# Output projection of a hybrid attention layer: gate folded into the weights, scale and shift in one VectorE instruction, three group-norm steps moved from GpSimd to VectorE

## The chip, the cores and the metric

The kernel runs on one core of one Trainium2 chip. The metric is the device time of one execution in microseconds (us); lower is better. Besides the time, one execution is recorded by the hardware profiler, and all rows below come from that record.

## The reference, cut to what matters

One layer: attention and retention heads are computed from a projected input, their outputs are concatenated and projected by `w_out`, the result is gated and added to the input, and the sum is normalised, modulated and sent to a mixture of experts.

```python
def _ret_output(o, gn_g, gn_b, gate, dtype):
    mu = jnp.mean(o, axis=-1, keepdims=True)
    var = jnp.mean(jnp.square(o - mu), axis=-1, keepdims=True)
    on = (o - mu) * lax.rsqrt(var + EPS)
    on = jnp.transpose(on, (0, 2, 1, 3)).reshape(B, L, H * dv).astype(dtype)
    return (on * gn_g + gn_b) * jax.nn.silu(gate)
...
    x_new = x + gt1 * (jnp.concatenate([attn_x, ret_x], axis=-1) @ w_out[l])
    h2 = _modulate(_rmsnorm(x_new, norm2_g[l]), sh2, sc2)
    y = _hier_moe(h2..., ...)
    x_new = x_new + gt2 * y
```

2048 tokens, width 1024, 4 retention heads of 128 values, 8 attention heads of 64, 32 experts in 4 groups of which each token takes two.

## The kernel before, in words

Everything is float32. Tokens lie on the 128 partitions, so there are 16 token tiles. Matrix products are made of three passes on rounded parts (high by high, high by low, low by high).

There are four stages. The first projects the input. The second (`phase2`, some 545 to 1268 us in the record) is attention: 288 steps, each with score products on TensorE, an exponential and a cast on ScalarE (ACT), a subtraction shared by VectorE (DVE) and GpSimd (POOL) (line 950), row maxima on DVE for units that come later (lines 900 and 905), and the products with the values. Its instruction order is written out by hand. Every third step it also takes one step of `fillers`, which prepares the third stage: it loads the modulation rows into `mod2` (gate, shift, scale; `mod2[:, 0]` is the gate gt1), loads `w_out` in 16 pieces of 128x512, splits each into a high and a low part (ACT line 1015, DVE line 1016), scans the retention states, loads constants, and runs the cross part of retention for token tile 0 (`cross_ahead`).

The third stage (`phase3`, 1268 to 1556 us) is the output projection with the second norm and the router. For each of the 16 tiles and each half of 512 columns, `wout` makes 24 matmuls into PSUM, multiplies the result by the gate (DVE line 1255, into a scratch tile `y3`) and adds it to `x` (DVE line 1256). `squares` takes the sum of squares on ACT (line 1277), `scaled` multiplies `x` by the norm's gain and modulation on DVE (line 1273, into `xa`). `norm2` computes the reciprocal root on small columns, multiplies `xa` by it on ACT (line 1283), adds the shift on POOL (line 1284) and stores `h2`. `h2_T` transposes `xa` on TensorE (line 1291) and copies it from PSUM on ACT (line 1292); `router` multiplies it by the router weights (line 1296); for every second tile `route` picks the experts of two tiles with some forty small DVE instructions (lines 1308 to 1373) and two on ACT (lines 1316 and 1349), then POOL scatters the choices into lists in memory (line 1376).

Beside that, two tiles ahead, `ret_cross` finishes the retention of a tile: a product on TensorE (line 1161), an addition and statistics on DVE, a normalisation by four ACT instructions (line 1176), and then three steps on POOL: times the gain (line 1180), plus the bias (line 1182), times the gate `gs` (line 1184). `mix_T` transposes the result for the projection of the next tile (line 1242).

Work of the third stage is put into slots (`self.at`, `self.flush`), and a scheduler orders the instructions of each engine when the program is built; on the chip each engine takes its own in that fixed order. PSUM tiles of the name `pr` share three buffers: the two transposes of `h2_T`, one of `mix_T` and the retention product follow each other through them. The SBUF tiles of the stage are reserved in a fixed order, `y3` third among them (two buffers of 2 KB per partition), on the space that the second stage leaves. SP issues nearly all loads and stores, in order.

The fourth stage computes the experts from 1589 us on. It starts from the lists and from `h2`.

Of the kernel before, what the change touches and what calls it, by code (L numbers as in the profile page):

```python
# [11 lines left out]
F32 = mybir.dt.float32  # L12
F32R = mybir.dt.float32r
F16 = mybir.dt.float16
I32 = mybir.dt.int32
AF = mybir.ActivationFunctionType
ALU = mybir.AluOpType
# [4 lines left out]
P = 128  # L22
D = 1024
KD = D // P
# [44 lines left out]
RING3 = {"qr": 3, "st": 3, "ro": 4, "gs3": 3, "bs": 1, "x3": 3}  # L69
# [63 lines left out]
class Build:  # L133
# [657 lines left out]
    def phase2(self):  # L791
# [10 lines left out]
        with tc.tile_pool(name="kv", bufs=1, reuse_waits="tile") as kv, tc.tile_pool(name="p2", bufs=2, reuse_waits="tile") as pool, \  # L802
# [186 lines left out]
            def fillers():  # L989

                g = self.mod2
                for j, dst in enumerate((g[:, 0, :], g[:, 1, :], g[:, 2, :], self.gt2)):
                    nc.sync.dma_start(dst, self.bcast(self.mod_d[:, j * D:(j + 1) * D], D))
                for j in range(2):
                    s_ = slice(j * 512, (j + 1) * 512)
                    n2 = p.tile([P, 512], F32, name="n2", tag="wa2", bufs=4)
                    nc.sync.dma_start(n2, self.bcast(a["norm2_g"][:, s_], 512))
                    yield
                    yield
                    nc.vector.scalar_tensor_tensor(g[:, 2, s_], g[:, 2, s_], 1.0, n2, op0=ALU.add, op1=ALU.mult)  # L1000
                pieces = [(k, n) for k in range(KD) for n in range(2)]
                raws = []
                for q in range(len(pieces) + 2):
                    if q < len(pieces):
                        k, n = pieces[q]
                        raw = p.tile([P, 512], F32, name="wor", tag="wa2", bufs=4)
                        nc.sync.dma_start(raw, a["w_out"][0, k * P:(k + 1) * P, n * 512:(n + 1) * 512])
                        raws.append(raw)
                    yield
                    if q < 2:  # L1010
                        continue
                    k, n = pieces[q - 2]
                    raw = raws[q - 2]
                    s_ = slice(n * 512, (n + 1) * 512)
                    nc.scalar.copy(self.wohi[:, k, s_], raw)
                    nc.vector.tensor_sub(self.wolo[:, k, s_], raw, self.wohi[:, k, s_])
                    yield

                gch = p.tile([P, RH], F32, name="gch", bufs=1)
                nc.scalar.activation(gch, self.gam[:, 8:12], AF.Exp, scale=float(P))  # L1020
                us = []
                for n in range(NT + 2):
                    if n < NT:
                        u = p.tile([P, RH, RV], F32, name="su", tag="wa2", bufs=4)
                        nc.sync.dma_start(u[0:64].rearrange("p h d -> p (h d)"), self.st_d[n, 0:64])
                        nc.sync.dma_start(u[64:128].rearrange("p h d -> p (h d)"), self.st_d[NT - 1 - n, 64:128])
                        us.append(u)
                    yield
                    if n < 3:
                        continue  # L1030
                    n -= 2
                    for h in range(RH):
                        nc.vector.scalar_tensor_tensor(us[n][:, h, :], us[n - 1][:, h, :], gch[:, h:h + 1], us[n][:, h, :], op0=ALU.mult, op1=ALU.add)
                    nc.sync.dma_start(self.st_d[n, 0:64], us[n][0:64].rearrange("p h d -> p (h d)"))
                    nc.sync.dma_start(self.st_d[NT - 1 - n, 64:128], us[n][64:128].rearrange("p h d -> p (h d)"))
                    yield

                for dst, src in ((self.list_d, a["slot_init"]), (self.acc_d[L:], a["zeros"]), (self.h2_d[L:], a["zeros"])):
                    nc.sync.dma_start(dst, src)
                    yield  # L1040
                for _ in self.constants3(p):
                    yield
                for t in range(AHEAD):
                    yield from self.cross_ahead(p, ps, t)
# [108 lines left out]
        nc.vector.tensor_mul(qx, pq, self.consts3[0])  # L1153
        return qx

    def ret_cross(self, alloc, psr, qx, st, o, gs):

        nc, gng = self.nc, self.consts3[1]
        pc = psr("pc3", [P, RH, RV])
        for h in range(RH):  # L1160
            nc.tensor.matmul(pc[:, h, :], qx[:, h, :], st[:, h, :], start=True, stop=True)
        nc.vector.tensor_add(o, pc, o)
        yield
        bs = alloc("bs", [P, RH, 6])
        mv = alloc("mv", [P, 5, RH, 2])
        for h in range(RH):
            nc.vector.bn_stats(bs[:, h, :], o[:, h, :])
        yield
        for h in range(RH):
            nc.vector.bn_aggr(mv[:, 0, h, :], bs[:, h, :])  # L1170
        rsqrt = self.rsqrt_steps(mv[:, 1, :, 0], mv[:, 0, :, 1], 1.0, (mv[:, 2, :, 0], mv[:, 3, :, 0]))
        yield from rsqrt
        nc.vector.scalar_tensor_tensor(mv[:, 4, :, 0], mv[:, 0, :, 0], -1.0, mv[:, 1, :, 0], op0=ALU.mult, op1=ALU.mult)
        yield
        for h in range(RH):
            nc.scalar.activation(o[:, h, :], o[:, h, :], AF.Identity, bias=mv[:, 4, h, 0:1], scale=mv[:, 1, h, 0:1])
            if h % 2:
                yield
        of = o.rearrange("p h d -> p (h d)")
        nc.gpsimd.tensor_mul(of, of, gng[:, 0, :])  # L1180
        yield
        nc.gpsimd.tensor_add(of, of, gng[:, 1, :])
        yield
        nc.gpsimd.tensor_mul(of, of, gs)

    def cross_ahead(self, p, ps, t):

        def alloc(name, shape, dt=F32):
            if name == "ro":
                return self.c3.tile(shape, dt, name=f"ro{t}")  # L1190
            if name in ("bs", "mv"):
                return p.tile(shape, dt, name=name, bufs=1)
            return p.tile(shape, dt, name=name, tag="wa2", bufs=4)

        def psr(name, shape, dt=F32):
            return ps.tile(shape, dt, name=name, tag="nm")

        qr, st, o, gs = self.ret_load(alloc, t)
        yield
        yield  # L1200
        qx = self.ret_T(alloc, psr, qr)
        yield
        yield from self.ret_cross(alloc, psr, qx, st, o, gs)
        self.crossed.append(o)
        yield

    def phase3(self):
        nc, tc, a = self.nc, self.tc, self.a
        with tc.tile_pool(name="p3", bufs=2, reuse_waits="tile") as pool, tc.tile_pool(name="ps3", bufs=2, space=PSUM, reuse_waits="tile") as ps:
            wr, br, ri, before, one16, run = self.consts3[2:]  # L1210

            p = Reserved(pool)
            for name, cols, dt in (("h2", D, F32), ("h2T", (KD, P), F32), ("y3", 512, F32), ("mThi", (KD, P), F32R), ("mTlo", (KD, P), F32R), ("xa", D, F32),
                                   ("x3", D, F32), ("qx", (RH, P), F32), ("mx3", H * HD, F32), ("qr", (RH, 2, HD), F32), ("st", (RH, RV), F32),
                                   ("ro", (RH, RV), F32), ("gs3", RH * RV, F32), ("en", (2, 2, 2), I32), ("ad", (2, 2), I32)):
                p.reserve(name, [P, *cols] if isinstance(cols, tuple) else [P, cols], dt, bufs=RING3.get(name, 2))
# [30 lines left out]
            def wout(hi, lo, n, x):  # L1247
                o = ps.tile([P, 512], F32, name="pw", tag="pw", bufs=3)
                for k in range(KD):
                    for i, (l, r) in enumerate(((hi, whi), (hi, wlo), (lo, whi))):  # L1250
                        ins = nc.tensor.matmul(o, l[:, k, :], r[:, k, n * 512:(n + 1) * 512], start=(k == 0 and i == 0), stop=(k == KD - 1 and i == 2))
                self.flush()
                s_ = slice(n * 512, (n + 1) * 512)
                y = p.tile([P, 512], F32, name="y3", bufs=RING3.get("y3", 2))
                nc.vector.tensor_mul(y, o, self.mod2[:, 0, s_])
                nc.vector.tensor_add(x[:, s_], y, x[:, s_])

            def shift_logits():

# [19 lines left out]
            def norm2(t, x, xa, h2, ss):  # L1279
                nc.sync.dma_start(self.acc_d[t * P:(t + 1) * P, :], x)  # L1280
                nc.vector.tensor_add(ss[:, 0:1], ss[:, 4:5], ss[:, 5:6])
                self.rsqrt(ss[:, 1:2], ss[:, 0:1], 1.0 / D, (ss[:, 2:3], ss[:, 3:4]))
                nc.scalar.activation(h2, xa, AF.Copy, scale=ss[:, 1:2])
                nc.gpsimd.tensor_add(h2, h2, self.mod2[:, 1, :])
                nc.sync.dma_start(self.h2_d[t * P:(t + 1) * P, :], h2)

            def h2_T(h2, h2T, half):
# [101 lines left out]

            def stage_cross(t):  # L1390
                if t < NT:
                    for _ in self.ret_cross(alloc, psr, R.pop((t, "qx")), *R[t][1:4]):
                        pass

            def stage_mix(t, half):
# [668 lines left out]
```

## Time and profile before

| what | us |
|---|---|
| median of 3 runs | 2432.54 |
| lowest and highest of them | 2430.21, 2434.29 |
| the profiled execution | 2424.75 |
| its span, first to last instruction | 2423.0 |
| third stage, of that span | 1268 to 1556 |
| from there to the first expert work on TensorE | 1556 to 1589 |

PE is TensorE's matmuls, PEld its weight loads, SPq the queue of SP. In a row of the timeline the first number is the start, the second the duration, both in us; what stands in brackets at its end is the idle time of that engine before it and what ended it. In a group of instructions the two numbers after the bar are the busy time in us and the mean duration in ns, those after the second bar the idle time before. L1284 is line 1284 of the kernel before.

### The profile page before, as it was taken

What the parts mean: (1) busy time and instruction counts of PE and PEld (TensorE: products, weight loads), DVE (VectorE), ACT (ScalarE), POOL (GpSimd) and SP (SyncE); (2) the same over time, 40 slices, a digit from 0 to 9 for tenths busy, and PEclk for the clock granted to TensorE, in tenths of its full rate; (3) what the DMA queues carried; (4) which work ended last, traced back from release to release, by engine and by line L of the source; (5) the groups of instructions that cost most, each with busy time, mean ns of one, the idle gap of its engine ahead of it and who ended that gap; (6) DMA issues with size and microseconds to landing.
All of it is one profiled execution on the core that took longest, in us unless ns stands there. A gap on an engine that the chain in (4) does not pass through costs nothing. (4 is left out here: it accounts for less than half of the span.)

```text
span 2423.0 us, 46706 instructions
## 1 busy us (share of the span) xinstructions
PE 2268.9 (94%) x16778; PEld 1835.5 (76%) x16778; DVE 1862.3 (77%) x3449; ACT 1510.5 (62%) x2179; POOL 951.3 (39%) x943
## 2 busy tenths in 40 slices
PE   7899999999999999999999998769999999999992
PEld 3788888886788877878877777557888787778872
DVE  6655555556888989998967888758878988887786
ACT  3533333333899999999984333345756766665663
POOL 2544444442455565556564445312232212121221
PEclk8999999998999999999999999889999999999996
DMA  7333444448011122223118544177887998897887
GB/s 273 104 111 113 116 118 118 118 134 221 24 41 41 45 54 58 63 60 99 31 64 268 156 150 136 73 227 253 296 299 260 361 332 302 316 358 236 281 296 294
DMA packets 221685, 417.88 MB, mean 172 GB/s; under 512 B 63931, under 2 KB 115427, under 8 KB 220211
## 3 DMA queue, kind: packets, MB, share of 16 engines
q1 hardware_dynamic: 186002, 363.00, 43.5%
q0 software_dynamic: 26672, 51.04, 9.0%
q8 instruction: 162, 2.65, 0.4%
q10 hardware_dynamic: 8736, 0.27, 0.2%
q14 instruction: 113, 0.92, 0.1%
HBM read 336.97 MB, written 86.23 MB: 175 GB/s over the span
## 5 line engine op out<-in xcount | busy, mean ns | idle before, releaser
L1536 DVE TENSOR_TENSOR wlo<-wraw,whi 128x1024 fp32r<-128x1024 f32 x384 | 460.0, 1246 | 28.4 <-ACT whi L1535 7.0
L950 POOL TENSOR_TENSOR pl<-p,ph 128x512 f16<-128x512 f32 x288 | 339.1, 1178 | 303.2 <-DVE pl L950 222.2
L1535 ACT CAST whi<-wraw 128x1024 fp32r<-128x1024 f32 x384 | 382.4, 1052 | 31.7 <-DMA wraw<-in_moe_w_gate 9.7
L905 DVE TENSOR_REDUCE mx<-sm 128x1 f32<-128x512 f32 x512 | 345.0, 685 | 62.9 <-PE sm L904 61.8
L1599 PE MATMUL gu<-whi,xT 128*128 128x512 f32 x1024 | 326.7, 395 | 5.9 <-DVE xT L1591 2.8
L938 ACT ACTIVATE p<-st,cexp 128x1024 f32<-128x1024 f32 x288 | 320.7, 1113 | 17.2 <-PE st L936 8.4
L942 ACT CAST ph<-p 128x1024 f16<-128x1024 f32 x288 | 301.6, 1047 | 7.5
L434 PE MATMUL pp<-whi,hT_hi 128*128 128x512 f32 (+1 forms) x688 | 263.1, 382 | 5.5 <-ACT v L625 3.3
L965 PEld LDWEIGHTS <-ph 128*128 128x128 f16 x4608 | 218.2, 97 | 65.7 <-issue 60.5
L434 PE MATMUL pp<-whi,hT_lo 128*128 128x512 f32 (+1 forms) x688 | 256.3, 373 | 2.7 <-POOL hT_lo L413 1.5
L434 PE MATMUL pp<-wlo,hT_hi 128*128 128x512 f32 (+1 forms) x688 | 255.1, 371 | 0.9 <-DVE wlo L388 0.9
L965 PE MATMUL o<-vx,ph 128*128 128x65 f16 (+1 forms) x4608 | 252.1, 194 | 1.3 <-ACT ob L971 1.2
L965 PE MATMUL o<-vx,pl 128*128 128x65 f16 x2304 | 239.8, 192 | 0.0
L904 PE MATMUL sm<-KHL,qhh 128*128 128x512 f32 x512 | 230.4, 455 | 5.6 <-DVE mx L905 2.8
L935 PE MATMUL st<-qhh,KHL 128*128 128x512 f32 x576 | 231.6, 402 | 1.0 <-ACT p L938 0.2
L1599 PEld LDWEIGHTS gu<-whi,xT 128*128 128x128 f32 x1024 | 193.9, 189 | 50.2 <-issue 6.1
L936 PE MATMUL st<-qlm,KO 65*128 65x512 f32 x576 | 231.8, 402 | 0.1
L1599 PE MATMUL Y<-whi,hT 128*128 128x512 f32 x624 | 216.8, 403 | 9.8 <-DVEq L1589 3.3
L950 DVE TENSOR_TENSOR pl<-p,ph 128x514 f16<-128x514 f32 x288 | 212.0, 736 | 15.9 <-ACT ph L942 11.2
L965 PEld LDWEIGHTS <-pl 128*128 128x128 f16 x2304 | 214.2, 99 | 0.0
L1599 PE MATMUL gu<-wlo,xT 128*128 128x512 f32 x512 | 200.7, 392 | 0.0
L1661 POOL DMA_INDIRECT acc_d<-y,slots x31 | 67.7, 2185 | 223.0 <-DVE y L1647 120.7
(354 smaller groups left out, 4610.0 us busy)
## 6 DMA issues: line engine op xcount, KB each, us to landing
wraw<-in_moe_w_gate SPq DMA_DIRECT2D x128, 512.0 KB
wraw<-in_moe_w_up SPq DMA_DIRECT2D x128, 512.0 KB
wraw<-in_moe_w_down SPq DMA_DIRECT2D x128, 512.0 KB
wa<-in_w_ada SPq DMA_DIRECT2D x64, 256.0 KB
wa<-in_w_ada SPq DMA_DIRECT2D x8, 1024.0 KB
wraw<-in_w_in SPq DMA_DIRECT2D x32, 256.0 KB
xt<-in_x SPq DMA_DIRECT2D x16, 512.0 KB
qh_d<-qt SPq DMA_DIRECT2D x64, 128.0 KB
```

The costliest lines, as they stand in the source:

```text
L434: ins = nc.tensor.matmul(out[:, :n], l[:, k, :], r[:, k, c0:c0 + n], start=(k == 0 and i == 0), stop=(k == KD - 1 and i == 2))
L904: nc.tensor.matmul(sm, qhh[:, h0 + h, j * P:(j + 1) * P], khl[g][:, n * 512:(n + 1) * 512], start=True, stop=True)
L905: nc.vector.reduce_max(mx[u][:, 2 * h + j, n:n + 1], sm, axis=AX.X)
L935: nc.tensor.matmul(st[:, n, :], khl[g][:, kt * P:(kt + 1) * P], qh, start=True, stop=False)
L936: nc.tensor.matmul(st[:, n, :], ko[g][:, kt * P:(kt + 1) * P], ql, start=False, stop=True)
L938: nc.scalar.activation(P32[i], st, AF.Exp, bias=cexp)
L942: nc.scalar.copy(PH[i], P32[i])
L950: eng.tensor_sub(out[:, a:b], x[:, a:b], hi[:, a:b])
L965: nc.tensor.matmul(o[:, a_, 0:m], l[:, n, s_], r, start=kt == 0 and a_ == 0 and l is ph and m > HD, stop=kt == NTT - 1 and l is pl, skip_g ...
L1535: nc.scalar.copy(hi, raw)
L1536: nc.vector.tensor_sub(lo, raw, hi)
L1599: nc.tensor.matmul(out, l[:, k].rearrange("p a n -> p (a n)")[:, 0::2] if a_ is None else l[:, k, a_, :], w[r], start=(k == 0 and i == 0), ...
```

## The change

Three edits. The gate gt1 is multiplied into each piece of `w_out` before it is split, in `fillers`, by 16 instructions on DVE; `wout` then adds the product straight from PSUM to `x`, and `y3` goes. The scale on ACT and the shift on POOL in `norm2` become one DVE instruction with a per-partition scalar and two tensors. The last three steps of `ret_cross` are issued on the engine that the caller names: DVE from `phase3` (tiles 1 to 15), POOL as before from `cross_ahead` (tile 0).

```diff
                 for q in range(len(pieces) + 2):
+                    if 1 <= q <= len(pieces):
+                        n = pieces[q - 1][1]
+                        nc.vector.tensor_mul(raws[q - 1], raws[q - 1], g[:, 0, n * 512:(n + 1) * 512])
                     if q < len(pieces):
...
-    def ret_cross(self, alloc, psr, qx, st, o, gs):
+    def ret_cross(self, eng, alloc, psr, qx, st, o, gs):
...
-        nc.gpsimd.tensor_mul(of, of, gng[:, 0, :])
+        eng.tensor_mul(of, of, gng[:, 0, :])
         yield
-        nc.gpsimd.tensor_add(of, of, gng[:, 1, :])
+        eng.tensor_add(of, of, gng[:, 1, :])
         yield
-        nc.gpsimd.tensor_mul(of, of, gs)
+        eng.tensor_mul(of, of, gs)
...
-        yield from self.ret_cross(alloc, psr, qx, st, o, gs)
+        yield from self.ret_cross(self.nc.gpsimd, alloc, psr, qx, st, o, gs)
...
-            for name, cols, dt in (("h2", D, F32), ("h2T", (KD, P), F32), ("y3", 512, F32), ("mThi", (KD, P), F32R), ...
+            for name, cols, dt in (("h2", D, F32), ("h2T", (KD, P), F32), ("mThi", (KD, P), F32R), ...
...
-                y = p.tile([P, 512], F32, name="y3", bufs=RING3.get("y3", 2))
-                nc.vector.tensor_mul(y, o, self.mod2[:, 0, s_])
-                nc.vector.tensor_add(x[:, s_], y, x[:, s_])
+                nc.vector.tensor_add(x[:, s_], o, x[:, s_])
...
-                nc.scalar.activation(h2, xa, AF.Copy, scale=ss[:, 1:2])
-                nc.gpsimd.tensor_add(h2, h2, self.mod2[:, 1, :])
+                nc.vector.scalar_tensor_tensor(h2, xa, ss[:, 1:2], self.mod2[:, 1, :], op0=ALU.mult, op1=ALU.add)
...
-                    for _ in self.ret_cross(alloc, psr, R.pop((t, "qx")), *R[t][1:4]):
+                    for _ in self.ret_cross(nc.vector, alloc, psr, R.pop((t, "qx")), *R[t][1:4]):
```

## Rows read from the trace of the kernel before

**Rows 1.** The page: the span, and the busy time of TensorE.
```profile
span 2423.0 us, 46706 instructions
...
PE 2268.9 (94%) x16778; PEld 1835.5 (76%) x16778; DVE 1862.3 (77%) x3449; ACT 1510.5 (62%) x2179; POOL 951.3 (39%) x943
```
**Rows 2.** Stretches: length, busy PE PEld DVE ACT POOL, granted clock, DMA share, GB/s.
```profile
1268.00:1556.00 288.00, 266.13 (x1491) 224.58 (x1491) 230.20 (x756) 110.61 (x278) 128.63 (x90) 0.98 0.50 163
1390.00:1410.00 20.00, 17.04 (x91) 14.35 (x90) 16.84 (x63) 8.15 (x22) 6.57 (x4) 0.91 0.59 198
...
1556.00:1589.00 33.00, 3.11 (x22) 2.11 (x21) 19.50 (x69) 8.80 (x14) 13.76 (x12) 0.58 0.45 158
```
**Rows 3.** TensorE's waits in 1268 to 1556: total us, times, longest.
```profile
PE pc L1161 <- ACT h2T L1292: 18.7, 6, 3.6
PE pl L1296 <- ACT h2T L1292: 1.6, 1, 1.6
PE pq L1151 <- DMA qr<-qr_d: 1.0, 1, 1.0
```
**Rows 4.** Timeline of one routing tile, 1395 to 1404.
```profile
1395.43 1.29 POOL L1184 TENSOR_TENSOR ro<-ro,gs 128x512 f32<-128x512 f32 x1
1395.47 1.80 DVE L1273 TENSOR_TENSOR xa<-x,mod 128x512 f32<-128x512 f32 x1
...
1399.86 2.37 POOL L1284 TENSOR_TENSOR h<-h,mod 128x1024 f32<-128x1024 f32 x1 [3.14 <-ACT h L1283]
...
1400.06 2.25 DVE L1335 SCALAR_TENSOR_TENSOR em<-O,em 128x64 f32<-128x64 f32 x1
...
1402.60 0.23 DVE L1330 TENSOR_TENSOR em<-em,sm 128x64 f32<-128x64 f32 x1
...
1402.93 0.20 ACT L1349 ACTIVATE sm<-sm 128x2 f32<-128x2 f32 x1 [3.15 <-DVE sm L1348]
...
1403.04 1.05 ACT L1292 COPY h2T<-ph 128x512 f32<-128x512 f32 x2
...
1403.66 0.60 PE L1161 MATMUL pc<-st,qx 128*128 128x128 f32 x3 [2.96 <-ACT h2T L1292]
```
**Rows 5.** Groups by line in 1268 to 1556, VectorE.
```profile
L1256 DVE TENSOR_TENSOR x<-y,x 128x512 f32<-128x512 f32 x31 | 33.5, 1081 | 0.4
L1273 DVE TENSOR_TENSOR xa<-x,mod 128x512 f32<-128x512 f32 x31 | 30.0, 967 | 0.3
...
L1255 DVE TENSOR_TENSOR y<-pw,mod 128x512 f32<-128x512 f32 x31 | 21.4, 689 | 33.0 <-PE pw L1251 27.1 <-issue 3.9 <-DMA wraw<-in_moe_w_gate 2.0
```
**Rows 6.** Two lines: duration in ns, min/median/max, and first and last start.
```profile
L1000 DVE SCALAR_TENSOR_TENSOR mod<-mod,n x2: 681/682/683, 647.9 to 661.3; 128x512 f32<-128x512 f32 x2
...
L1536 DVE TENSOR_TENSOR wlo<-wraw,whi x384: 1205/1217/2079, 1571.0 to 2366.2; 128x1024 fp32r<-128x1024 f32 x192
```
**Rows 7.** Timeline from the last projection to the first expert tile.
```profile
1556.75 0.69 DVE L1255 TENSOR_TENSOR y<-pw,mod 128x512 f32<-128x512 f32 x1 [0.73 <-PE pw L1251]
...
1562.62 2.90 DVE L1322 TENSOR_TENSOR ge<-ge,sm 128x4 f32<-128x4 f32 x1
1563.14 2.35 POOL L1284 TENSOR_TENSOR h<-h,mod 128x1024 f32<-128x1024 f32 x1
...
1588.77 1.98 PE L1573 MATMUL tr<-ident,xg 128*128 128x128 f32 x8 [19.42 <-DMA xg<-h_d,slots]
```
**Rows 8.** The split of w_out in the second stage, and TensorE's waits in 680 to 890.
```profile
L1016 DVE TENSOR_TENSOR wolo<-wor,wohi x16: 679/692/1582, 681.8 to 888.3; 128x512 fp32r<-128x512 f32 x16
...
PE sm L904 <- DVE mx L900: 1.6, 3, 0.5
```
**Rows 9.** Start of the third stage: SP's first load of x, GpSimd's last attention output.
```profile
1262.45 0.33 SPq L1232 DMA_DIRECT2D x<-in_x  x1
...
1270.63 1.09 POOL L984 TENSOR_TENSOR ob<-ob,rd 128x512 f32<-128x512 f32 x1
```
**Rows 10.** Timeline: the four normalisations of one tile on ScalarE.
```profile
1427.73 1.65 ACT L1176 ACTIVATE ro<-ro,mv 128x128 f32<-128x128 f32 x4 [0.83 <-DVE mv L1173]
```

More of the change, by code (lines that the diff above doesn't have):

```diff
@@ L1212, in phase3 @@
             p = Reserved(pool)
-            for name, cols, dt in (("h2", D, F32), ("h2T", (KD, P), F32), ("y3", 512, F32), ("mThi", (KD, P), F32R), ("mTlo", (KD, P), F32R), ("xa", D, F32),
+            for name, cols, dt in (("h2", D, F32), ("h2T", (KD, P), F32), ("mThi", (KD, P), F32R), ("mTlo", (KD, P), F32R), ("xa", D, F32),
                                    ("x3", D, F32), ("qx", (RH, P), F32), ("mx3", H * HD, F32), ("qr", (RH, 2, HD), F32), ("st", (RH, RV), F32),
```

## The prediction

> **What bounds the kernel now.** I read the page first: TensorE is busy for 2268.9 of 2423.0 us [rows 1], so a gain has to come from its idle time, from a lower granted clock, or from work taken off it; the change takes no matmul away. Next the busy time by stretch. In the third stage, 288 us, TensorE is busy for 266.1, VectorE for 230.2, ScalarE for 110.6 and GpSimd for 128.6; after it come 33 us in which TensorE does 3.1 [rows 2]. Then TensorE's waits in that stage: nearly all of the idle 22 us is one kind of wait, the retention product (L1161) held up by ScalarE's copy of the transposed `xa` (L1292), 18.7 us in six places, and once the router product behind the same copy, 1.6 us [rows 3]. The six lie some 37 us apart, one in each pair of tiles: the tiles that route.
>
> The timeline of one of them tells why [rows 4]. The shift of the norm starts on GpSimd at 1399.86 and takes 2.37 us. VectorE's next instruction, a small one of 128x64, starts at 1400.06 and ends at 1402.31, when GpSimd does; a sister of the same size takes 0.23. VectorE's way to that point was already late: L1273 ran from 1395.47 for 1.80 us beside GpSimd's L1184, where 0.68 to 0.69 is the price of its shape when undisturbed [rows 6]. ScalarE's in-order queue has L1349, which needs the result of this small work, ahead of the copies: it sits idle for 3.15 us until 1402.93, copies from 1403.04, and TensorE, which needs the PSUM buffer that the first copy frees, starts at 1403.66 after 2.96 us of nothing. So VectorE is held by GpSimd, ScalarE by VectorE, TensorE by ScalarE. Without the two blocks (2.25 - 0.23 = 2.02 and 1.80 - 0.68 = 1.12, together 3.14) L1349 would have come at 1399.8, and the wait of 2.96 would be gone.
>
> The idle places have a second price: after four of the six the granted clock is at the lower of its two levels (1.2 instead of 2.4 GHz) for a short while. A stretch of 20 us around one shows 0.91 on the average [rows 2], so 0.09 x 20 = 1.8 us lost; four like it give about 7 us.
>
> **The sum, part by part.** The profiled execution took 2424.75 us with a span of 2423.0, which lies 7.8 below the median of 2432.54. I make the sum on this execution and put the difference to the median.
>
> First, what leaves VectorE in the third stage: 31 gate products of 0.689, 21.4 us [rows 5]; the excess of L1256, which will read PSUM like L1255 did and cost the same 0.69: 31 x (1.081 - 0.69) = 12.1; that of L1273: 31 x (0.967 - 0.68) = 8.9; and seven blocks like the one at L1335, 7 x 2.02 = 14.1. Together 56.5. That the excess goes is read from who was running: in the rows each slow instruction has two SBUF tensors as inputs and runs beside a GpSimd elementwise step, while L1255, with one of its inputs in PSUM, averages 0.689 over all 31 [rows 4, 5]. After the change GpSimd has no elementwise step left in the stage, but the last attention outputs at its start. What comes: three steps of 128x512 for 15 tiles, 45 x 0.68 = 30.7 us, and 16 fused instructions of 128x1024, which the trace does not show; the nearest row is a subtraction of that size with two SBUF inputs, median 1.217 [rows 6], and a fused instruction of 128x512 costs 0.682, no more than a plain one, so 16 x 1.22 = 19.5. Together 50.2. VectorE ends up no busier than now. ScalarE loses 16 instructions (L1283), GpSimd all its long ones; neither was at its limit.
>
> **TensorE's waits in the third stage.** Now 20.3 us in seven places [rows 3]. If all new VectorE work of a tile stood ahead of L1349, it would come 3 x 0.68 + 1.22 - 0.69 = 2.57 later than without blocks, and 2.57 of the 3.14 would be given back: a wait of 2.4 would stay. If the scheduler puts the copies ahead, or the new work behind, nothing stays. The retention steps are needed only by the next tile and `h2` only in the fourth stage, so both can stand behind; ScalarE has also one instruction less to do ahead of the copies. I take 0.7 us for each place, nearer to nothing: 20.3 - 4.9 = 15.4 gained (bounds 3.5 and 20.3). The clock: at waits this short I expect no fall, since the stage has none outside the places after the long waits: 7.0 gained (bounds 3.5 and 7.0).
>
> **The tail, 1556 to 1589.** This is one chain: the last half, the norm, the last route, the scatter, the load of the lists, the gather [rows 7]. The gate product leaves it: 0.7. L1322 ends with the last shift on GpSimd after 2.90; an instruction of its kind takes some 0.2 [rows 4], so 2.7 is the block. The fused instruction gives back between nothing and its 1.22, as it stands behind or ahead of the last route; I take the middle, 0.6. Gain 0.7 + 2.7 - 0.6 = 2.8 (bounds 2.2 and 3.4). `h2` is stored earlier, but the gather waits for the lists.
>
> **The second stage.** 16 new products of 128x512 with two SBUF inputs run where TensorE has almost no idle time. They take the filler steps in which no split stood, since each piece takes two steps. The twin is L1016: 13 of 16 ran in 0.68 to 0.69, three took about 1.57 [rows 8], and behind those three alone TensorE waited, 1.6 us in all. The cover is VectorE's own idle time there, which hid the other thirteen; the cost is nothing if the products are not held, and 16 x 0.53 = 8.5 if each is. A gain is excluded, as only work is added. I take 0.5: one product in 16 held.
>
> The trace first: of 16 like instructions GpSimd held three [rows 8]. The Trainium skill, SBUF — State Buffer, section "SBUF: two separate sides", says that a VectorE instruction with two SBUF inputs and a GpSimd one that reads SBUF exclude each other for their whole length. GpSimd subtracts in every step of that stage, so the rule taken alone could hold every product: the sum would end 8 us later, at the upper end above.
>
> **The start of the third stage.** With `y3` gone, all tiles behind it lie 4 KB lower. By the sizes in the code, the first buffer of `x3` then falls on the small tile `rd`, which GpSimd reads until 1271.7; its load was issued at 1262.45 [rows 9], and SP's queue has the loads for tile 2 behind it. Issued 9 us later, they arrive before the first half is summed or up to 5 us late. Gain at most the 1.0 that TensorE waits for such a load [rows 3]. I take 1.5.
>
> Sum: -15.4 - 7.0 - 2.8 + 0.5 + 1.5 = -23.2. From 2424.75 to 2401.6 in a like execution, from the median 2432.54 to 2409.3.
>
> **Rivals.** *VectorE fills the room.* The new work stands ahead of L1349 in every routing tile: 2.4 us stay, of the clock half. -3.5 - 3.5 - 2.2 + 2 = -7.2: 2425. For it: VectorE is busy for 80% of the stage [rows 2]. Against: the scheduler orders by readiness, and the retention steps become ready in the middle of the tile.
>
> *The block moves instead of going.* If the moved steps meet GpSimd work that reads SBUF, or hold it up, only the tail's gain stays, less the 2.0 of the other stages: -2.8 + 2.0, 2432. Against: nothing elementwise is left there, only list scatters. The Trainium skill, Perfetto Trace Analysis, "Optimizing Scalar/DVE Operations", warns that moving work between these two may not help as they share a read port; the rows show the shared cost, and that here it leaves with its second user.
>
> *Two queues wait for each other* (slower). The first of the three steps needs all four normalisations, 1.65 us on ScalarE [rows 10]. In VectorE's order it may stand right behind the statistics; VectorE then stands still, and the next half's addition, the copy for the projection and the route stand behind it, while ScalarE's own queue may stand behind L1349 for 3.15 us [rows 4]. VectorE's idle time is 58 us in 16 tiles, 3.6 each; the work itself is level, so it decides from 3.6 us of such waits per tile on. 1.65 + 3.15 = 4.8 is 1.2 over: 15 x 1.2 = 18, less 2.8 in the tail: 2448.
>
> **Chances.** Forecast 0.68, the room filled 0.14, the block moved 0.09, the mutual wait 0.09. The prediction is the forecast's 2409.3. With all terms at their good ends it would be 2432.5 - 20.3 - 7.0 - 3.4 - 1.0 = 2400.8; the range goes from 2400 up over the filled room to 2430. A measurement of this kernel tells 0.2% (some 5 us, below 2427.7) from no change: faster 0.79 (the filled room is just inside for the most part), same 0.12, slower 0.09.
>
> **What would show it.** L1256's successor and L1273 at 0.69 throughout; the small instruction of L1335 at 0.2; the fused one at 1.2; TensorE's wait for L1292 under 5 us in all; no low clock between 1268 and the end of the stage, which is some 22 us shorter; the tail near 30 us. A wait of TensorE for the low part of the projection's input, or of VectorE for L1176 above 3 us a tile, would make it wrong, as would new waits for VectorE's maxima at 680 to 890.

## The result, and the profile after

The changed kernel takes 2404.43 us, median of 4 runs (2402.05 to 2406.26), beside 2431.38 for the kernel before in the same comparison: ratio 0.990, with a 95% interval of 0.9883 to 0.9918, so 20 to 28 us faster. Its profiled execution took 2402.05 against 2424.75 before [rows 1]: 22.7 less.

Lines after line 1002 are moved by up to four: L1251 before is L1255 after, L1256 is L1258, L1273 is L1275, L1335 is L1336, L1349 is L1350, L1292 is L1293, L1161 is L1165. In the experiments below a line number is that of the run's own kernel. The fused instruction is L1285, the gate product on the weights L1007, the three moved steps L1184, L1186 and L1188.

The page of the changed kernel, to be read beside [rows 1]:

```profile
span 2400.3 us, 46625 instructions
...
PE 2264.6 (94%) x16778; PEld 1833.5 (76%) x16778; DVE 1845.2 (77%) x3494; ACT 1493.6 (62%) x2163; POOL 854.0 (36%) x882
```

Its third stage, a stretch around a routing tile, and the tail; length, then busy PE, PEld, DVE, ACT, POOL, the granted clock, DMA share and GB/s, as in [rows 2]:

```profile
1268.00:1536.00 268.00, 260.80 (x1495) 221.39 (x1493) 204.46 (x786) 95.52 (x263) 34.67 (x31) 0.99 0.54 178
1536.00:1568.00 32.00, 3.35 (x20) 2.54 (x18) 17.43 (x68) 7.58 (x13) 11.92 (x11) 0.58 0.47 163
1390.00:1410.00 20.00, 20.00 (x126) 17.35 (x125) 17.74 (x71) 7.76 (x22) 0.00 (x0) 1.00 0.53 172
```

From the start of the projection's first matmul to the start of its last the stage went from 288.1 to 267.3 us; from there to the first expert transpose it took 32.1 instead of 32.5. The fourth stage went from 834.2 to 832.3, which lies in the spread of the kernels below (832 to 837, with that stage the same in all), and the first two stages by 0.4 the other way. So practically the whole gain is in the third stage. The 20 us around 1400 had 2.96 us without matmuls and a granted clock of 0.91; now TensorE is busy throughout at 1.00.

TensorE's waits in that stage (total, times, longest), against [rows 3]:

```profile
PE pq L1155 <- DMA qr<-qr_d: 6.8, 1, 6.8
PE pw L1255 <- ACT mThi L1248: 0.3, 1, 0.3
```

The 20.3 us behind ScalarE's copies are gone to the last one. One new wait stands in the list, 6.8 us for a load. VectorE's groups there, against [rows 5]:

```profile
L1258 DVE TENSOR_TENSOR x<-pw,x 128x512 f32<-128x512 f32 x31 | 21.4, 691 | 16.2 <-PE pw L1255 15.9 <-DMA x<-in_x 0.3
L1275 DVE TENSOR_TENSOR xa<-x,mod 128x512 f32<-128x512 f32 x31 | 21.3, 688 | 0.3
L1285 DVE SCALAR_TENSOR_TENSOR h<-xa,ss,mod 128x1024 f32<-128x1024 f32 x15 | 19.2, 1282 | 0.3
...
L1184 DVE TENSOR_TENSOR ro<-ro,gng 128x512 f32<-128x512 f32 x15 | 10.3, 687 | 12.0 <-ACT ro L1180 12.0
```

The addition fell from 1081 to 691 ns and the scaling from 967 to 688. The fused instruction costs 1282. A routing tile in the timeline (start, duration), against [rows 4]:

```profile
1398.40 1.03 PE L1292 MATMUL ph<-ident,xa 128*128 128x128 f32 x8
...
1399.04 1.07 ACT L1293 COPY h2T<-ph 128x512 f32<-128x512 f32 x2 [2.09 <-PE ph L1292]
...
1399.71 1.12 PE L1165 MATMUL pc<-st,qx 128*128 128x128 f32 x8
...
1403.77 0.22 DVE L1336 SCALAR_TENSOR_TENSOR em<-O,em 128x64 f32<-128x64 f32 x1
...
1404.68 0.20 ACT L1350 ACTIVATE sm<-sm 128x2 f32<-128x2 f32 x1 [0.89 <-DVE sm L1349]
```

Two things differ from before. The small instruction of the route takes 0.22 instead of 2.25. And ScalarE's order has turned round: the copies come 5.6 us ahead of the route's L1350, behind which they stood before. The retention product follows the copy without a gap. Whether the gone block or the turned order made the gain, the comparison can't tell: the change brought both.

The new wait, at the start of the stage, against [rows 9]:

```profile
1270.94 1.08 POOL L984 TENSOR_TENSOR ob<-ob,rd 128x512 f32<-128x512 f32 x1
...
1272.06 0.33 SPq L1236 DMA_DIRECT2D x<-in_x  x1
...
1272.94 1.20 SPq L1142 DMA_DIRECT2D qr<-qr_d  x2
...
1278.28 1.09 PE L1155 MATMUL pq<-ident,qr 128*128 128x128 f32 x4 [6.76 <-DMA qr<-qr_d]
```

The load of `x` is issued at 1272.06 instead of 1262.45, when GpSimd has read `rd` for the last time; the loads of `qr` queue behind it, and TensorE stands for 6.76 us. Behind the wait the granted clock is at the lower level until 1281.8.

The tail, against [rows 7]:

```profile
1536.73 0.96 POOL L1377 DMA_INDIRECT list_d<-en,ad  x1 [0.30 <-issue]
...
1539.98 0.17 DVE L1356 TENSOR_SCALAR en<-ri 128x2 int32<-128x2 f32 x1 [1.99 <-DMA list_d<-en,ad]
...
1540.55 0.57 ACT L1293 COPY h2T<-ph 128x512 f32<-128x512 f32 x1
...
1541.17 1.92 PE L1297 MATMUL pl<-wr,h2T 128*128 128x36 f32 x8 [2.60 <-ACT h2T L1293]
...
1567.94 1.98 PE L1574 MATMUL tr<-ident,xg 128*128 128x128 f32 x8 [19.71 <-DMA xg<-h_d,slots]
```

The block of 2.90 us is gone from it, but VectorE now stands for 1.99 at L1356. This writes `en`, one of two buffers, from which a scatter issued at 1536.73 is still reading. The last norm stands behind it.

### The profile page after: what moved, and what is told of

It is laid out like the page before. It is cut to its first block, busy times and chain, and to the rows that moved or that the text cites. A ratio compares the mean times of both kernels' runs of the same rounds, so it can differ in the third digit from the quotient of the medians.

```text
span 2400.3 us, 46625 instructions
## 1 busy us (share of the span) xinstructions
PE 2264.6 (94%) x16778; PEld 1833.5 (76%) x16778; DVE 1845.2 (77%) x3494; ACT 1493.6 (62%) x2163; POOL 854.0 (36%) x882
## 5 line engine op out<-in xcount | busy, mean ns | idle before, releaser
L950 POOL TENSOR_TENSOR pl<-p,ph 128x512 f16<-128x512 f32 x288 | 338.9, 1178 | 305.2 <-DVE pl L950 227.7
L950 DVE TENSOR_TENSOR pl<-p,ph 128x514 f16<-128x514 f32 x288 | 212.8, 739 | 16.3 <-ACT ph L942 12.9
L434 PEld LDWEIGHTS pp<-whi,hT_hi 128*128 128x128 f32 x688 | 131.2, 191 | 30.6 <-ACT v L625 3.7
```

Of the source, the lines that this page charges most:

```text
L434: ins = nc.tensor.matmul(out[:, :n], l[:, k, :], r[:, k, c0:c0 + n], start=(k == 0 and i == 0), stop=(k == KD - 1 and i == 2))
L950: eng.tensor_sub(out[:, a:b], x[:, a:b], hi[:, a:b])
```

## The experiments

Two theories of the same loss. A: GpSimd's elementwise steps hold VectorE's instructions with two SBUF inputs. B: the order of ScalarE's queue, with L1349 ahead of the copies, makes of a late VectorE a late TensorE; whatever turns that order cures it. The stage is measured from the start of the first projection matmul to the start of the last, the tail from there to the first expert transpose; both come from each run's trace.

| kernel | median us | ratio to before, 95% interval | stage | tail |
|---|---|---|---|---|
| before | 2426.5 to 2431.4 | 1 | 288.1 | 32.5 |
| changed | 2404.43 | 0.990 (0.9883 to 0.9918) | 267.3 | 32.1 |
| b1_memset | 2399.86 | 0.9878 (0.9851 to 0.9905) | 263.0 | 30.7 |
| d1_pool_reads | 2407.62 | 0.9913 (0.9886 to 0.9939) | 270.2 | 31.9 |
| d2_pool_writes | 2397.59 | 0.9874 (0.9854 to 0.9894) | 260.6 | 31.9 |
| p1_fused_only | 2399.87 | 0.9882 (0.9862 to 0.9902) | 262.0 | 31.7 |
| p2_ret_only | 2411.67 | 0.9931 (0.9911 to 0.995) | 273.4 | 32.6 |
| p3_gate_only | 2426.65 | 0.999 (0.9974 to 1.0005) | 288.1 | 32.8 |
| e1_hole_kept | 2397.05 | 0.987 (0.9843 to 0.9897) | 259.0 | 31.8 |
| e2_hole_en3 | 2394.4 | 0.9854 (0.9828 to 0.9881) | 258.9 | 30.2 |
| e3_no_fold | 2394.1 | 0.9853 (0.9836 to 0.9869) | 260.3 | 30.7 |
| e4_no_ret | 2396.57 | 0.9867 (0.985 to 0.9883) | 259.9 | 30.1 |

### The start: the room of `y3` kept, and a third `en`

```diff
-("h2T", (KD, P), F32), ("mThi"
+("h2T", (KD, P), F32), ("y3", 512, F32), ("mThi"
```

The changed kernel with the room of `y3` still reserved, though nothing uses it:

> The changed kernel with the two 2 KB buffers of y3 still reserved in their old place, though nothing uses them. Theory: with y3 gone the first x tile fell on rd, SP's queue stood until GpSimd had read it, and TensorE waited 6.8 us for the loads of tile 2 and ran some 3.5 us at the lower clock after it. With the hole the load is issued near 1262 again, that wait falls to 1 us or less, and the time to 2404.4 - 5.8 - 1.7 = about 2397. Rival: the loads were late for another cause (traffic of the weight loads beside them): the wait stays and the time is 2404.

2397.05. The wait of 6.8 us and the low clock behind it are gone, the load of `x` is issued at 1263.86, the stage is 8.3 us shorter, the median 7.4 us. So this was the price of moving the tiles, and of nothing else in the change. Then, with that, a third buffer:

```diff
-en = tile2("en", (2, 2, 2), I32, bufs=2)
+en = tile2("en", (2, 2, 2), I32, bufs=3)
```

> As e1_hole_kept, and a third buffer for en, the tile from which GpSimd scatters the choices. Theory: in the changed kernel VectorE stands still for 2.0 us in the tail at L1356, which rewrites the en buffer of an earlier route before its scatter has landed; this ate the tail's gain. With a third buffer that wait is gone and the time is 2.0 below e1_hole_kept: about 2395. Rival: the scatters on GpSimd, one after the other, set the end of the tail, and the time is that of e1_hole_kept.

2394.4. The wait at L1356 is gone and the tail 1.6 us shorter than in e1. In time the two can't be told apart; the trace shows the 1.6. This kernel is ahead of the kernel before and of the changed one: the intervals of the two ratios don't overlap, and the medians lie 10 us apart. Its stage and tail in the view of [rows 2]:

```profile
1268.00:1530.00 262.00, 261.54 (x1579) 222.69 (x1575) 204.18 (x784) 96.02 (x264) 35.27 (x31) 1.00 0.55 183
1530.00:1561.00 31.00, 4.23 (x23) 3.20 (x22) 17.97 (x73) 7.69 (x13) 11.39 (x11) 0.56 0.48 168
```

TensorE is busy for 261.54 of 262 us at full clock: no wait and no low clock is left to be won in this stage.

### Block or order

The kernel before with GpSimd's shift replaced by a fill, which leaves the norm's scale and shift out of `h2`. The order of PE, DVE and ACT stays that of the kernel before.

```diff
-nc.gpsimd.tensor_add(h2, h2, self.mod2[:, 1, :])
+nc.gpsimd.memset(h2, 0.0)
```

> The kernel before with the shift of the norm on GpSimd (L1284) replaced by a fill of h2 with zeros, which reads nothing; h2 is then zero, so the expert products are of zeros, while the choices stay as they are. The order of all other engines is that of the kernel before, with ScalarE's L1349 ahead of the copies. Theory A (GpSimd's reading step blocks VectorE): L1335 falls from 2.25 to 0.22, TensorE's seven waits from 20.3 to about 7 x 0.9 = 6 us (L1273 is still held by L1184), the low clock goes (7) and L1322 in the tail (2.7): about 2431.4 - 14 - 7 - 2.7 = 2408. Theory B (only the order in ScalarE's queue counts): L1335 may or may not change, the waits stay for the most part: 2425 to 2431. If a fill blocks like a reading step, nothing changes: 2431.

2399.86: B alone falls. A alone had said 2408, with 6 us of waits behind the copies left; 1.8 us were left behind L1161, and L1273, which was expected to be held as before, fell from 967 to 741 ns. A routing tile in its timeline:

```profile
1391.16 0.96 POOL L1284 MEMSET h<- 128x1024 f32 x1 [3.37 <-ACT h L1283]
1391.38 0.23 DVE L1335 SCALAR_TENSOR_TENSOR em<-O,em 128x64 f32<-128x64 f32 x1
...
1392.22 0.20 ACT L1349 ACTIVATE sm<-sm 128x2 f32<-128x2 f32 x1 [1.12 <-DVE sm L1348]
...
1392.33 1.05 ACT L1292 COPY h2T<-ph 128x512 f32<-128x512 f32 x2
...
1392.95 1.16 PE L1161 MATMUL pc<-st,qx 128*128 128x128 f32 x8 [0.36 <-ACT h2T L1292]
```

L1335 runs in 0.23 beside the fill, L1349 still stands ahead of the copies, and TensorE waits 0.36 where it waited 2.96. But a fill is also shorter (0.96 against 2.4 us), so the next pair puts either kind into the kernel with the room kept, where the order is the new one: a tile `junk` in place of `y3`, written once for every token tile, by an addition that reads two SBUF tiles, or by two fills. The fills read nothing and so wait for nothing, and they did not run where the additions did: all 32 ran one behind the other from 1280.99 to 1313.37, ahead of the first route.

```diff
+junk = p.tile([P, D], F32, name="junk", bufs=1)
+nc.gpsimd.tensor_add(junk, xa, self.mod2[:, 1, :])   # d1_pool_reads
+nc.gpsimd.memset(junk, 0.0)                          # d2_pool_writes, twice
```

> The changed kernel with an added GpSimd addition of 128x1024 per tile, of xa and the shift, into a scratch tile of 4 KB that lies where y3 was (so the hole of e1_hole_kept is kept; compare with that). ScalarE's order is that of the changed kernel, with the copies ahead of L1350. Theory A alone: the blocks of VectorE come back, about 2 us in each tile, and TensorE's waits with them, some 14 us in the seven routing tiles and the lower clock after a part: e1_hole_kept + 15 to 20. Theory B: with the copies ahead the blocks reach nobody: e1_hole_kept + 0 to 3 (the tail).

> As d1_pool_reads, but with two fills of the scratch tile (128x1024 each, about 1 us) in place of the addition: GpSimd is as busy but reads nothing. Theory A: no VectorE instruction is held by a fill, and the time is that of e1_hole_kept. If a fill held VectorE too, the durations of the small VectorE instructions beside it would show 1 us more.

The addition costs 10.6 us against e1, between the two theories; the fills cost 0.5, nothing that can be measured. As no fill stood at a routing tile, the time of d2 says nothing of the routing tiles; what it can show is what happens beside a fill. The addition in the timeline, and the instructions that were held (groups, busy us and mean ns):

```profile
1375.63 2.40 POOL L1287 TENSOR_TENSOR junk<-xa,mod 128x1024 f32<-128x1024 f32 x1 [14.66 <-DVE ss L1283]
...
1375.79 2.26 DVE L1376 TENSOR_TENSOR ad<-ev 128x4 int32<-128x4 f32 x1
```

```profile
L220 DVE TENSOR_TENSOR ss<-ss 128x1 f32<-128x1 f32 x15 | 13.4, 892 | 2.1 <-ACT ss L218 1.2
...
L1376 DVE TENSOR_TENSOR ad<-ev 128x4 int32<-128x4 f32 x6 | 11.4, 1904 | 0.0
```

Two places among the fills of d2, the timelines of GpSimd and VectorE put together:

```profile
1290.17 0.95 POOL L1288 MEMSET junk<- 128x1024 f32 x1
1290.25 0.16 DVE L220 TENSOR_TENSOR ss<-ss 128x1 f32<-128x1 f32 x1 [0.50 <-ACT ss L218]
1290.83 1.28 DVE L1285 SCALAR_TENSOR_TENSOR h<-xa,ss,mod 128x1024 f32<-128x1024 f32 x1
1291.18 0.95 POOL L1287 MEMSET junk<- 128x1024 f32 x1
...
1301.29 0.96 POOL L1287 MEMSET junk<- 128x1024 f32 x1
1301.34 0.92 DVE L215 TENSOR_SCALAR mv<-mv 128x4 f32<-128x4 f32 x1
```

L220, on 128x1 with two SBUF inputs, was held by seven of the additions, up to 1.77 us; its mean is 892 ns. Beside a fill it ran only twice, in 0.16 each. In the 32.4 us of the fills, of which GpSimd is busy for 30.6, 29 VectorE instructions with two SBUF inputs ran beside one, and none took more than 0.01 us above its usual time: the moved steps 0.68 to 0.69, the fused instruction 1.28. In b1, where a fill stands in the place of the shift, all seven L1335 took 0.22 to 0.23. So for these it is the reading, not GpSimd's being busy. The Trainium skill, SBUF — State Buffer, section "Who interferes with whom", says the same: a VectorE instruction with two SBUF inputs contends with a GpSimd instruction that reads SBUF, not with one that only writes it. The rows of d1, d2 and b1 agree. One instruction with a single SBUF input was held as well, by fills too: L215 on 128x4 takes 0.16 to 0.17 us, up to 2.15 beside the shift in the kernel before, 0.64 to 0.67 beside five fills of b1, 0.42 and 0.92 beside two of d2. Why this one is held, the runs do not show.

With the new order ScalarE's copies no longer stand behind the held instructions, and a block costs less: at five routing tiles of d1 TensorE waits 0.46 to 0.52 us, not the 3 of [rows 4], and behind three of them the granted clock is 0.83 over 10 us, 1.7 us each.

### One part at a time

Each on the kernel before, with the room of `y3` as it was (used in the first two, unused in the third), and nothing else of the change; first the fused scale and shift alone:

> The kernel before with the fused scale and shift alone. The block at L1335 leaves, those of the three retention steps on GpSimd (at L1273 and L1256) stay, VectorE gets 1.22 us more per tile, and ScalarE's order turns: the copies now come ahead of L1349's successor. Theory A alone: waits of 2.96 - 2.02 + 1.22 = 2.2 stay in seven places: about 2431.4 - 5 - 3 - 2 = 2421. Theory B: the waits and the low clock are gone: 2431.4 - 20.3 - 7 - 1 = 2403.

2399.87: within 3 us of all three parts together with the room kept, and 3 below what theory B gave. In its trace the waits for the copies and the low clock of the routing tiles are gone, and ScalarE has the copies ahead of the route. L1256 and L1273 are still held by the retention steps (means of 933 and 843 ns), and no wait of TensorE comes of it. Its stage is 3.0 us longer than that of e1, all of it ahead of the routing tiles: waits of 0.36 us for a load and 0.94 for a copy at L1265, and behind them a granted clock of 0.83 from 1295 to 1305. Then the retention steps alone:

> The kernel before with the three retention steps on VectorE alone. The shift stays on GpSimd and blocks L1335 for 2 us; ScalarE's order turns as in p1_fused_only. Theory A alone: only the 1.1 us at L1273 leaves and 2.05 come: the waits stay near 20 us: 2428 to 2433. Theory B: the waits and the low clock are gone while L1335 still takes 2.25: 2404 to 2406.

2411.67, between the theories again. Its ScalarE has the new order too, but for the last routing tile of the stage, and its GpSimd still adds the shift:

```profile
1364.06 2.37 POOL L1284 TENSOR_TENSOR h<-h,mod 128x1024 f32<-128x1024 f32 x1 [10.89 <-issue]
...
1364.12 2.39 DVE L1331 TENSOR_TENSOR em<-em,ri 128x64 f32<-128x64 f32 x1
```

TensorE's waits from 1290 to 1533, and a place behind that, in the timeline:

```profile
PE pp L1342 <- DVE A L1337: 4.5, 6, 0.8
PE pc L1161 <- ACT h2T L1292: 3.0, 5, 0.6
```

```profile
1534.62 1.08 PE L1296 MATMUL pl<-wr,h2T 128*128 128x36 f32 x8 [1.69 <-ACT h2T L1292]
```

The block is there in full, on another instruction. What it costs has fallen from 3 us a pair of tiles to 0.60 and 0.76, and the clock does not fall there. In the last routing tile, where L1349 still stands ahead of the copies, L1335 is held for 2.30, TensorE waits 1.69, and the clock falls behind it (0.83 from 1535 to 1545). So with the order turned in the other six about half of the loss went while the shift still blocked: the stage lost 14.7 of the 29.1 us that lie between before and e1. As 45 reading steps left GpSimd with the same edit, the half isn't the order's alone; how it splits stays open. At last the gate folded, alone:

> The kernel before with the gate folded into the weights alone, y3 still reserved. ScalarE's order is the old one, with L1349 ahead of the copies; the blocks by L1184 and L1284 stay. Both theories: TensorE's waits stay; VectorE has 0.69 and the block of L1256 less ahead of the route, so each wait may shrink by up to 1 us: 2424 to 2431. The 16 products in the second stage cost 0 to 1.6 there.

2426.65 against 2428.45 for before: no difference that can be measured. The addition, now reading PSUM, is no longer held (688 ns), and others are:

```profile
L1274 DVE TENSOR_TENSOR xa<-x,mod 128x512 f32<-128x512 f32 x31 | 31.5, 1016 | 0.5
...
L1332 DVE TENSOR_TENSOR em<-em,ri 128x64 f32<-128x64 f32 x14 | 18.5, 1318 | 0.2
...
L1282 DVE TENSOR_TENSOR ss<-ss 128x1 f32<-128x1 f32 x15 | 10.9, 729 | 0.0
```

Before, these took 967, 224 and 219 ns. L1332 is held by the shift, in L1335's stead; L1282 by the retention steps, which before held the addition.

TensorE waits for the copies as before, 16.3 us in six places. The three parts alone give 28.6, 16.8 and 1.8, more in sum than all of them together (29.5 with the room kept): the first two cure one illness.

### All but one part

With the third `en`, and `y3` used or its room kept: first without the folding, then without the moved retention steps.

> The kernel before with the fused scale and shift, the retention steps on VectorE and a third `en` buffer; the gate stays a product of its own, through `y3`. If blocks by GpSimd's reading steps and ScalarE's order were the whole loss, VectorE's 21.4 us of gate products are off the path and the time is that of the kernel with the room of `y3` kept and three `en` buffers, 2394 to 2397, but for 0.7 in the tail. If the fold pays once the blocks are gone (VectorE, with 51 us more to do than the kernel before has without blocks, gets late), it is 2400 or more, with new waits of TensorE behind the copies and the additions.

> The kernel before with the fused scale and shift, the gate folded (room of `y3` kept) and a third `en` buffer; the three retention steps stay on GpSimd, where each reads two SBUF tiles for about 1.2 us. Theory of the blocks: 45 such steps hold the additions and the scaling (1.08 and 0.97 us for 0.69 without), but VectorE has 30 us less to do, so the time is 2396 to 2399. If moving the retention steps is what pays, 2405 or more.

2394.1 and 2396.57, both as e2 within their intervals. Without the folding VectorE does 32 products more in the stage and nobody waits for it. Without the moved steps it is held again, at other places than those that TensorE waits for; its groups in the stage:

```profile
L1274 DVE TENSOR_TENSOR xa<-x,mod 128x512 f32<-128x512 f32 x31 | 24.9, 802 | 0.5
...
L1282 DVE TENSOR_TENSOR ss<-ss 128x1 f32<-128x1 f32 x15 | 10.6, 707 | 0.5 <-ACT h L1278 0.5
```

So of the three edits one, the fused instruction, carries the gain. The other two add at most the 3.0 us by which the stage of p1 is longer than that of e1, and by the times nothing that can be told from zero. The moved steps alone gain 16.8, but nothing measurable on top of the fused instruction. Giving up `y3`, which the folding made possible, cost 7 to 8 us.

## Why the prediction was right, and where its terms were off

The forecast of 2409.3 and its mechanism held: GpSimd's steps held VectorE, VectorE ScalarE, ScalarE TensorE. In like executions the sum was -23.2, and the trace shows -22.7; by the medians the gain is 27.0, and 2404.43 lies 4.9 below the forecast. That the sum is so near is in part luck: three terms missed and cancelled, and 1.9 us come from the fourth stage, which the sum left out and which differs by as much between other runs.

*TensorE's waits*: -15.4 forecast, -20.3 measured, the good bound. I kept 0.7 for each place because I didn't know where the scheduler would put the copies. It put them ahead of L1350, by 5.6 us in the tile shown, and nothing stayed. b1 shows that with the block gone the old order leaves little as well, 1.8 us in five places.

*The clock*: -7.0 forecast. In the routing tiles it fell nowhere, and TensorE's busy time between the first and the last projection matmul went from 266.4 to 260.4: 6.0 less, or 7.7 without the 1.7 us newly lost at the start. The sign "no low clock between 1268 and the end of the stage" failed there. The argument, that waits this short bring no fall, was too simple: in d1 TensorE waited 0.52 at 1369.15, and the granted clock was 0.83 from 1370 to 1380, while p2 with 0.60 and 0.76 had no fall at such places. The term held because no waits stayed.

*The start of the third stage*: +1.5 forecast with 5 as the upper bound, some 8.5 measured (6.76 of waiting, 1.7 of low clock; e1 gives back 8.3). The step that failed is the sentence that the loads "arrive before the first half is summed or up to 5 us late". The shift onto `rd` and the time of issue were right (1272.06). I had looked at when `x` is needed; the first sufferer was the load of `qr` behind it, which TensorE needs at once, and I had not put the clock's fall behind such a wait.

*The tail*: -2.8 forecast, -0.4 measured. The block of 2.7 did go. In its place came the wait for `en`, 1.99 us: the tail's steps come closer together, and a scatter that had landed in time before is now late. I asked of the block where it went, and not what VectorE's next instruction would wait for.

*The second stage*: +0.5 forecast; its end moved by 0.3, and TensorE's waits there are the same three (1.6 us). The sixteen products, and the splits, three of which are held as in [rows 8] (min/median/max ns):

```profile
L1007 DVE TENSOR_TENSOR wor<-wor,mod x16: 681/681/683, 668.5 to 867.1; 128x512 f32<-128x512 f32 x16
...
L1020 DVE TENSOR_TENSOR wolo<-wor,wohi x16: 681/692/1581, 682.0 to 888.5; 128x512 fp32r<-128x512 f32 x16
```

None is held. One of them in the timeline shows why:

```profile
700.89 1.17 POOL L950 TENSOR_TENSOR pl<-p,ph 128x512 f16<-128x512 f32 x1 [0.81 <-DVE nm L911]
702.29 0.68 DVE L1007 TENSOR_TENSOR wor<-wor,mod 128x512 f32<-128x512 f32 x1
702.89 0.69 DVE L950 TENSOR_TENSOR pl<-p,ph 128x514 f16<-128x514 f32 x1
703.73 1.16 POOL L950 TENSOR_TENSOR pl<-p,ph 128x512 f16<-128x512 f32 x1 [1.67 <-DVE pl L950]
```

GpSimd's next subtraction waits for VectorE's own, and the product stands ahead of that: the two can't meet. None of the sixteen runs beside a GpSimd instruction in the trace, while the three slow splits each run beside an L950. The rule of the Trainium skill, SBUF — State Buffer, section "SBUF: two separate sides", by which each could have been held, agrees with the trace all the same: what it needs, an overlap, was missing.

*VectorE's load*: I counted 56.5 us going and 50.2 coming, so "no busier than now"; between the same two matmuls it fell from 230.0 to 203.9. Summed over all of VectorE's groups in the stage (by line, tiles and shape), the time above the shortest of each was 40.3 us, and the seven L1335, all held alike, add 14.2: 54.5, not the 35.1 that I had listed, since small ones such as L215 (7.2) and L1344 (4.7) were held too; 5.0 is left. It moved no time.

*The rivals*: the full room (2425) fell because the copies went ahead; the moved block (2432) because no elementwise step was left on GpSimd after the start of the stage; the mutual wait (2448) because VectorE waits for the normalisation, L1184 behind L1180, only 12.0 us over 15 tiles, 0.8 each, where 3.6 would have decided.

## What to carry to other kernels

Before moving work between engines, find out what the slow instruction overlaps with, and who stands behind it in an in-order queue: the sixteen fused instructions were worth more than the other two edits together, because the step that they replaced held the one small instruction that two queues waited for. When a tile is removed, look up what the tiles behind it now fall on, and which loads are queued behind the one that must wait; keeping 4 KB reserved was worth 7 to 8 us. Once TensorE is busy for all of a stage, VectorE's savings there buy nothing (e3), so look at the ends of the stage.

## What the hardware showed that I had not expected

A fill on GpSimd does not hold VectorE's instructions with two SBUF inputs (29 beside fills in d2, seven L1335 in b1), an addition does, and the size of the held instruction is no protection: 128x1 took up to 1.77 us instead of 0.16, and 128x4 some 2.25. But L215, with one SBUF input on 128x4, was held by every fill that it met, to 0.92 us at the most. Freeing one instruction from the block, by letting it read PSUM, hands the block to others: with the gate folded alone L1282, on 128x1, rose from 219 to 729 ns on the average, and the time stayed.
